# Input projection of a decoder layer: pairs of weight tiles, units of two row blocks, accumulators in three banks

## Chip, cores and metric

One NeuronCore of a Trainium2 chip runs the whole program. The metric is device microseconds of one execution. The time before is 1057.71 us, the median of three runs (1054.66 to 1057.97).

## The reference

One layer of a hybrid decoder, batch 1, 256 tokens, model width 2048, float32. A vector c gives six modulation vectors (shift, scale and gate for two sub-layers) through a matrix of 2048 x 12288. The normed and modulated input h goes through one input projection `w_in` of 2048 x 5144. Its columns feed four groups of eight heads of width 64: A (dilated windows), B (sliding window, two key heads, sinks), C (block sparse), D (compressed, selected and window attention with gates, two key heads). At 256 tokens these are causal attentions with different biases and masks. Each group's output is normed, the four are joined and go through the output projection `w_out` (2048 x 2048), gated into x. Then a router picks two of 16 experts (width 512) for each token, and a final norm follows.

```
mod = silu(c) @ ada_w + ada_b                  # sh1, sc1, g1, sh2, sc2, g2
h   = rmsnorm(x) * (1 + sc1) + sh1
q_a,k_a,v_a, q_b,k_b,v_b, q_c,k_c,v_c, q_d,k_dc,v_dc,k_ds,v_ds,k_dw,v_dw, g_d = split(h @ w_in)
x   = x + g1 * (concat(rmsnorm(o_a), rmsnorm(o_b), rmsnorm(o_c), rmsnorm(o_d)) @ w_out)
x   = x + g2 * moe(rmsnorm(x) * (1 + sc2) + sh2)
out = rmsnorm(x)
```

## The kernel before

All weights stream once from HBM as units of 512 KB (128 partitions x 1024 floats) through one list. `Stream` (L101) gives each unit the next free slot of a ring of 11 slots, to which two more are added when an attention group's bias tile is done (L990) and more when the attention's pool is closed (L1133). SyncE's queue issues all of these loads in the list's order; each waits until the former user of its slot is done.

**First stage.** Eight rounds (L606 to L634). Each round loads eight units of `ada_w` for sc1 and sh1 (256 columns, rows of 1 KB) and two early units of `w_in` (one row block of 128 rows by 1024 columns, rows of 4 KB, L253). It makes two row blocks of h as a high and a low half (`Hh`, `Hl`, L599), and multiplies the early units into four accumulators, D's first four tiles. A product in two halves is three matmuls (`three`, L534): low weight x high h, high x low, high x high. The weight's halves are made by `halves` (L555): a cast on ScalarE (L560) and a subtraction on VectorE (L562). Two more accumulators, "S" and "pv" (L565), take tile 4 (D's window keys) and three quarters of tile 6 (C's first keys); one unit of 4 row blocks x 256 columns of one of the two is loaded in each round but the first (L274 to L277).

**Second stage.** The input projection's other tiles, each of 256 columns as four units of 4 row blocks x 256 columns (rows of 1 KB, L205). The tiles' order is written out by hand (`wtiles`, L192): D's gates, then for C and for A the keys, values and queries of the first 256 columns and the same of the second, then B. One tile accumulates in one "mm" bank of PSUM, two in turn (L696). A unit is 24 matmuls of 256 columns: for keys and queries the weight is the stationary side (L537 to L539), for values h is (L541 to L543). After the last unit the tile is copied out by ScalarE (`evac`, L726). Between these units stand 96 units of `ada_w` of 4 KB rows that VectorE accumulates (`ada_acc_v`, L477, L484), spread over the list by L285 to L294.

The four attentions are generators. After each unit of the projection `step(PACE[m])` (L1087) adds a fraction to a credit; each whole point runs the front generator to its next yield (L1019). One full step of an attention (L978) computes scores of one item, transposes the probabilities of the item before and multiplies the values of the one before that. D's generator is queued at the first piece, the others behind the last unit of the first query tile of their group (L1088), and each waits where its second query tile is not yet there (L980).

**Output projection.** 32 units of `w_out` of 512 columns (L1212), three matmuls each for the halves, with the gate g1's 32 units of `ada_w` between them. Each unit lets `step(3)` run, so B's attention ends here. `WORDER` (L42) puts the twelve units of D, C and A for two column blocks ahead of B's first. At the fifth unit `attention_done` (L1124) closes the attention's buffers; loads into their memory wait for B's end. Then come the router, the gather (L1375) and eight pairs of experts.

The change touches `wtiles` and `win_units` (L192 to L208), the first stage (L274, L580 to L590, L626 to L637), `pieces`, `piece_mms` and `evac` (L652 to L762), the order of the first copies out and the queueing of the attentions (L1071, L1088) and `PACE` (L51).

## Time and profile before

| | us |
|---|---|
| median of three runs | 1057.71 |
| the profiled execution's own time | 1057.37 |
| its span, first to last instruction | 1055.6 |
| TensorE busy | 961.1 (91%) |
| VectorE busy | 499.2 (47%) |
| ScalarE busy | 350.0 (33%) |
| bytes moved | 371.18 MB, mean 352 GB/s |

How to read it: PE is TensorE's matmuls, PEld its weight loads, DVE is VectorE, ACT ScalarE, SP the queue of SyncE. A matmul's busy time contains its way through the pipeline, so matmuls overlap and their starts tell the pace. PEclk is the granted share of TensorE's clock. The DMA share is the mean busy share of 16 engines; it can read a little over 1. "idle before, releaser" is the time an instruction's engine stood idle ahead of it, and what ended it. A line such as L173 belongs to a helper that all matmul groups of a batch use, so groups are told apart by their tiles: `acc` is the input projection, `oacc` the output projection, `sp`, `PT` and `opv` are scores, transposes and values, `ada` modulation.

### The profile page before, as it was taken

How to read it: one execution, taken by the hardware profiler on the slowest of the kernel's cores; microseconds unless marked ns; L12 is line 12 of the kernel's file. 1: busy time of each engine (PE TensorE's matmuls, PEld its weight loads, DVE VectorE, ACT ScalarE, POOL GpSimd, SP SyncE). 2: the span in 40 equal slices, each digit the busy share in tenths (PEclk: the TensorE clock that was granted, in tenths of full speed). 3: DMA queues.
4: the chain of work that ended last, by engine and by line, in shares of the span. 5: the costliest groups of instructions: out<-in, count | busy, mean ns of one | idle time of the engine just before them, and what ended most of it. 6: DMA issues, size and time to landing. Idle time of an engine off the chain costs nothing.

```text
span 1055.6 us, 16579 instructions
## 1 busy us (share of the span) xinstructions
PE 961.1 (91%) x6433; PEld 581.7 (55%) x6433; DVE 499.2 (47%) x1008; ACT 350.0 (33%) x763; POOL 4.8 (0%) x14
## 2 busy tenths in 40 slices
PE   5899989999899998989998999999989897998884
PEld 1677778898788985646794435433343232432222
DVE  2444466996898998344444232414033130413115
ACT  3333345566776757534443101100020000200013
POOL 0000000000000000000000000000000000000000
PEclk9999999999999999989998999999999999999998
DMA  9999999996999999889743999999999999999994
GB/s 330 357 357 357 351 307 348 348 371 213 348 325 346 347 375 384 311 283 377 277 163 123 410 408 409 409 409 409 410 409 409 409 409 409 409 410 409 409 386 137
DMA packets 172031, 371.18 MB, mean 352 GB/s; under 512 B 13561, under 2 KB 92322, under 8 KB 171690
## 3 DMA queue, kind: packets, MB, share of 16 engines
q1 hardware_dynamic: 170944, 368.42, 95.0%
q10 hardware_dynamic: 938, 1.61, 0.4%
q8 instruction: 53, 0.87, 0.4%
q14 instruction: 32, 0.26, 0.1%
q0 software_dynamic: 64, 0.02, 0.0%
HBM read 367.91 MB, written 2.10 MB: 351 GB/s over the span
## 4 chain that ended last, share of the span: by engine, by line
PE 47%; DMA 37%; DVE 8%; ACT 4%; issue 3%; SPq 0%; ACTq 0%; DVEq 0%
DMA ugu<-in_exp_w_gate_dram 11%; DMA ugu<-in_exp_w_up_dram 10%; DMA udh<-in_exp_w_down_dram 6%; PE dn L170 6%; DMA uw<-in_w_in_dram 4%; PE acc L537 4%; PE acc L538 4%; PE acc L539 3%; PE ada L170 3%; DMA usc<-in_ada_w_dram 3%; PE oacc L541 3%; PE pg L1384 3%; PE oacc L543 3%; PE oacc L542 3%; PE gatep L170 2%
## 5 line engine op out<-in xcount | busy, mean ns | idle before, releaser
L537 PE MATMUL acc<-Hh,wlo 128*128 128x256 f32 x512 | 145.0, 293 | 7.3 <-DVE wlo L562 4.7
L538 PE MATMUL acc<-Hl,whi 128*128 128x256 f32 x512 | 145.2, 286 | 0.0
L539 PE MATMUL acc<-Hh,whi 128*128 128x256 f32 x512 | 144.4, 285 | 0.0
L173 PE MATMUL gatep<-ugu,xg 128*64 128x512 f32 x364 | 123.1, 600 | 0.0
L173 PE MATMUL upp<-ugu,xg 128*64 128x512 f32 x368 | 121.5, 596 | 0.0
L170 PE MATMUL dn<-udh,heT 128*64 128x512 f32 x242 | 112.1, 600 | 2.9 <-DVE heT L1454 2.6
L173 PE MATMUL dn<-udh,heT 128*64 128x512 f32 x234 | 108.3, 600 | 0.0
L537 PEld LDWEIGHTS acc<-Hh,wlo 128*128 128x128 f32 x512 | 95.6, 191 | 18.1 <-DVE wlo L562 7.7
L538 PEld LDWEIGHTS acc<-Hl,whi 128*128 128x128 f32 x512 | 97.8, 191 | 3.5 <-issue 3.0
L539 PEld LDWEIGHTS acc<-Hh,whi 128*128 128x128 f32 x512 | 97.7, 191 | 2.7 <-issue 2.3
L1437 DVE TENSOR_TENSOR he<-upp,sg 128x128 f32<-128x128 f32 x32 | 7.1, 284 | 171.0 <-PE upp L173 168.3
L562 DVE TENSOR_TENSOR wlo<-uw,whi 128x1024 fp32r<-128x1024 f32 x62 | 75.7, 1221 | 19.2 <-ACT whi L560 19.2
L170 PE MATMUL gatep<-ugu,xg 128*64 128x512 f32 x144 | 75.4, 612 | 7.8 <-DMA ugu<-in_exp_w_gate_dram 7.7
L170 PE MATMUL upp<-ugu,xg 128*64 128x512 f32 x144 | 73.9, 601 | 7.5 <-DMA ugu<-in_exp_w_up_dram 7.5
L560 ACT CAST whi<-uw 128x1024 fp32r<-128x1024 f32 x62 | 64.9, 1048 | 45.4 <-DMA uw<-in_w_in_dram 18.4
L1516 ACT CAST yhl<-yo 128x512 fp32r<-128x512 f32 x31 | 19.2, 618 | 159.5 <-DVE yo L1510 153.2
L1467 DVE TENSOR_TENSOR xt<-xt,sco 128x512 f32<-128x512 f32 (+1 forms) x70 | 42.3, 639 | 54.7 <-PE sco L1466 54.3
L170 PEld LDWEIGHTS dn<-udh,heT 128*64 128x64 f32 x242 | 30.0, 136 | 62.1 <-issue 48.8
L562 DVE TENSOR_TENSOR wlo<-uo,whi 128x1024 fp32r<-128x1024 f32 x31 | 37.8, 1223 | 51.0 <-ACT whi L560 51.0
L1433 ACT ACTIVATE sg<-gatep 128x512 f32<-128x512 f32 x8 | 4.8, 597 | 162.4 <-PE gatep L173 162.4
L541 PE MATMUL oacc<-wlo,Oh 128*128 128x512 f32 (+1 forms) x160 | 58.5, 367 | 0.1
L543 PE MATMUL oacc<-whi,Oh 128*128 128x512 f32 (+1 forms) x160 | 56.5, 353 | 0.0
(396 smaller groups left out, 1777.1 us busy)
## 6 DMA issues: line engine op xcount, KB each, us to landing
ugu<-in_exp_w_up_dram SPq DMA_DIRECT2D x128, 512.0 KB, 10.2
ugu<-in_exp_w_gate_dram SPq DMA_DIRECT2D x127, 512.0 KB, 10.2
udh<-in_exp_w_down_dram SPq DMA_DIRECT2D x119, 512.0 KB, 10.2
usc<-in_ada_w_dram SPq DMA_DIRECT2D x64, 512.0 KB, 8.6
ush<-in_ada_w_dram SPq DMA_DIRECT2D x62, 512.0 KB, 7.1
uw<-in_w_in_dram SPq DMA_DIRECT2D x62, 512.0 KB, 6.8
ug<-in_ada_w_dram SPq DMA_DIRECT2D x56, 512.0 KB, 7.0
uo<-in_w_out_dram SPq DMA_DIRECT2D x31, 512.0 KB, 9.1
```

Of the source, the lines that this page charges most:

```text
L170: ins = op(*args, **kw).ins
L173: ins = op(*args, **kw).ins
L537: ins = mm(o, wl, hh, start=first, stop=False)
L538: mm(o, wh, hl, start=False, stop=False)
L539: mm(o, wh, hh, start=False, stop=last)
L541: ins = mm(o, hh, wl, start=first, stop=False)
L542: mm(o, hl, wh, start=False, stop=False)
L543: mm(o, hh, wh, start=False, stop=last)
L560: A.copy(hi, w)
L562: V.tensor_tensor(lo, w, hi[:].bitcast(F32), OP.subtract)
L1384: mm(pg[:, i, :], x_[:, t, i, 128 * c:128 * c + 128], oh4[q][:, t].rearrange("p e s -> p (e s)"), start=n == 0, stop=n == 3)
L1467: V.tensor_tensor(y(t, cs), y(t, cs), o, OP.add)
```

## The change

The tiles of C, A and B's queries become pairs of 512 columns, loaded as eight units of 2 row blocks x 512 columns (rows of 2 KB). A pair has two accumulators, one for each 256 columns of keys or queries, or for each 128 tokens of values; a value unit is then 12 matmuls of 512 columns. Accumulators take the banks "ada", "mm", "mm" in turn. C's keys, one unit in each of the eight rounds, take the place of tiles 4 and 6 in the first stage; D's window keys (four units of rows of 1 KB, like B's keys) come behind the gates. A pair's first tile is copied out ahead of the second's matmuls of the last unit. An attention is queued behind the last unit of its query pair. The pace goes from 0.65 to 0.7 for C and from 0.5 to 0.45 for A.

```
-PACE = {"D": 0, "C": 0.65, "A": 0.5, "B": 0.8}
+PACE = {"D": 0, "C": 0.7, "A": 0.45, "B": 0.8}
...
-              ("D", "kw", 0, 4864), ("D", "g", 0, 5120)]
-    for m, q0 in (("C", 2304), ("A", 0)):
-        for j in range(2):
-            wtiles += [(m, kind, j, q0 + off + 256 * j) for kind, off in (("k", 512), ("v", 1024), ("q", 0))]
-    wtiles += [("B", "kb", 0, 2048), ("B", "q", 0, 1536), ("B", "q", 1, 1792)]
+              ("C", "k", None, 2816), ("D", "g", 0, 5120), ("D", "kw", 0, 4864),
+              ("C", "v", None, 3328), ("C", "q", None, 2304),
+              ("A", "k", None, 512), ("A", "v", None, 1024), ("A", "q", None, 0),
+              ("B", "kb", 0, 2048), ("B", "q", None, 1536)]
+
+    def wparts(i):
+        return 1 if wtiles[i][1] == "g" else 8 if wtiles[i][2] is None else 4
...
+        n = wparts(i)
+        kn, w = 16 // n, 64 * n
         def mk(u):
             return lambda t: nc.sync.dma_start(
-                t.rearrange("p (k n) -> p k n", k=4), winT[:, 4 * u:4 * u + 4, col:col + 256])
-        return [((("w", i), u), mk(u)) for u in range(4)]
+                t.rearrange("p (k n) -> p k n", k=kn), winT[:, kn * u:kn * u + kn, col:col + w])
+        return [((("w", i), u), mk(u)) for u in range(n)]
...
-        if j % 2:
-            units.append(win_units(4)[j // 2])
-        elif j:
-            units.append(win_units(SIXTH)[j // 2 - 1])
+        units.append(win_units(NEARLY - 1)[j])
...
+    def early_mms2(u):
+        hi, lo = [a.rearrange("p (k n) -> p k n", k=2) for a in esp.pop(("pair", u))]
+        for i in range(2):
+            for cc in range(2):
+                c0 = 256 * i + 128 * cc
+                for kk in range(2):
+                    k = 2 * u + kk
+                    three(early[4 + i][:, cc, :], hi[:, kk, c0:c0 + 128], lo[:, kk, c0:c0 + 128],
+                          Hh[:, k, :], Hl[:, k, :], False, k == KC - 1 and cc == 1, True)
...
         if j:
             early_mms(2 * j - 1)
-        if j and j % 2 == 0:
-            early_mms5(4, j // 2 - 1)
+            early_mms2(j - 1)
         early_split(2 * j + 1)
...
+        early_split2(j)
     for k in (14, 15):
         early_mms(k)
-    early_mms5(4, 3)
+    early_mms2(7)
...
         if u == 0:
-            acc_banks[i] = ps("mm", [128, 2, 256], name="acc")
...
+            acc_banks[i] = []
+            for _ in range(tiles):
+                acc_banks[i].append(ps(("ada", "mm", "mm")[len(turn) % 3], [128, 2, 256], name="acc"))
+                turn.append(1)
+        for tj in range(tiles):
+            bank_ = acc_banks[i][tj]
+            if kind == "v":
+                ts = slice(128 * tj, 128 * tj + 128)
+                for kk in range(kn):
+                    k = kn * u + kk
+                    three(bank_[:].rearrange("p c n -> p (c n)"), hv[:, kk, :], lv[:, kk, :], Hh[:, k, ts], Hl[:, k, ts],
+                          k == 0, k == KC - 1, False)
+            else:
...
+                        ins = three(bank_[:, cc, :], hv[:, kk, c0:c0 + 128], lv[:, kk, c0:c0 + 128], Hh[:, k, :], Hl[:, k, :],
+                                    first, k == KC - 1 and cc == 1, True)
...
+            if u == nu - 1:
+                evac(i, tj)
...
-    for i in (2, 0, 1, 3, 4):
-        evac(i)
+    for i, tj in ((2, 0), (4, 1), (0, 0), (1, 0), (3, 0), (4, 0)):
+        evac(i, tj)
...
-            if u == 3 and wtiles[i][1:3] == ("q", 0) or pn == 1:
+            if u == 7 and wtiles[i][1] == "q" or pn == 1:
                 side.append(attention(m))
```

## Rows read from the trace of the kernel before

**Rows 1.** Windows by stage: us, busy by engine (instructions), PEclk, DMA share, GB/s
```profile
0.00:150.00 150.00, 127.25 (x1451) 90.27 (x1451) 64.08 (x161) 53.62 (x107) 2.05 (x9) 0.99 1.04 341
160.00:400.00 240.00, 231.19 (x1968) 204.72 (x1968) 208.58 (x380) 153.94 (x367) 1.05 (x2) 1.00 0.97 336
400.00:550.00 150.00, 140.63 (x813) 98.76 (x811) 73.85 (x141) 71.77 (x150) 1.70 (x3) 0.97 0.84 298
...
580.00:1030.00 450.00, 414.51 (x1886) 157.48 (x1884) 114.01 (x228) 42.93 (x72) 0.00 (x0) 0.99 1.03 407
```

**Rows 2.** Narrower windows, the same columns
```profile
50.00:100.00 50.00, 47.39 (x562) 35.58 (x561) 22.97 (x52) 17.48 (x34) 0.00 (x0) 1.00 1.08 356
...
400.00:430.00 30.00, 26.11 (x146) 16.46 (x144) 19.80 (x51) 19.36 (x54) 0.00 (x0) 0.94 1.04 382
...
470.00:480.00 10.00, 10.00 (x41) 4.02 (x34) 1.79 (x2) 2.10 (x4) 0.00 (x0) 0.74 1.03 388
...
560.00:570.00 10.00, 10.00 (x44) 4.58 (x45) 4.32 (x11) 2.77 (x5) 0.00 (x0) 0.81 0.01 2
```

**Rows 3.** Timeline of TensorE in the input projection: start us, us, instruction
```profile
257.81 0.28 PE L537 MATMUL acc<-Hh,wlo 128*128 128x256 f32 x1
257.93 0.28 PE L538 MATMUL acc<-Hl,whi 128*128 128x256 f32 x1
```

**Rows 4.** Waits of TensorE, 160 to 400 us, three largest: total us, times, longest
```profile
PE acc L537 <- DVE wlo L562: 4.7, 5, 1.7
PE PT L173 <- ACT prob L932: 1.0, 1, 1.0
PE acc L541 <- DVE wlo L562: 1.0, 1, 1.0
```

**Rows 5.** Groups by line and form, 160 to 460 us: busy, mean ns, idle before, releasers
```profile
L562 DVE TENSOR_TENSOR wlo<-uw,whi 128x1024 fp32r<-128x1024 f32 x54 | 65.9, 1221 | 17.9 <-ACT whi L560 17.9
...
L560 ACT CAST whi<-uw 128x1024 fp32r<-128x1024 f32 x54 | 56.5, 1047 | 43.3 <-DMA uw<-in_w_in_dram 18.4 <-PE acc L539 11.4 <-issue 3.7
```

**Rows 6.** Timeline of TensorE in the output projection
```profile
437.89 0.40 PE L541 MATMUL oacc<-wlo,Oh 128*128 128x512 f32 x1
438.12 0.39 PE L542 MATMUL oacc<-whi,Ol 128*128 128x512 f32 x1
```

**Rows 7.** Timeline of TensorE around one attention step
```profile
406.70 0.33 PE L170 MATMUL PT<-ident,prob 128*128 128x128 f32 x1
406.87 0.71 PE L173 MATMUL PT<-ident,prob 128*128 128x128 f32 x5
407.50 0.93 PE L173 MATMUL sp<-qkB 64*128 64x128 f32 x8
408.36 0.62 PE L170 MATMUL ada<-ug,cB 128*32 128x512 f32 x1
...
409.36 0.43 PE L170 MATMUL opv<-probT,vB 128*64 128x256 f32 x1
...
410.16 0.50 PE L541 MATMUL oacc<-wlo,Oh 128*128 128x512 f32 x1
```

**Rows 8.** Timelines of TensorE, then VectorE: B's attention, the projection's end
```profile
389.69 0.37 PE L170 MATMUL sp<-qkB 64*128 64x128 f32 x1
...
400.38 0.28 PE L539 MATMUL acc<-Hh,whi 128*128 128x256 f32 x1
...
425.69 0.93 PE L173 MATMUL sp<-qkB 64*128 64x128 f32 x8
...
433.54 0.93 PE L173 MATMUL sp<-qkB 64*128 64x128 f32 x8
...
462.60 1.43 DVE L1103 TENSOR_TENSOR Ol<-oT,Oh 128x256 fp32r<-128x256 f32 x4
```

**Rows 9.** Timeline of TensorE behind the twelfth output unit
```profile
465.99 0.37 PE L1147 MATMUL bb<-wbs,ones 128*128 128x16 f32 x2 [1.84 <-DVE wbs L1145]
469.75 1.06 PE L170 MATMUL ada<-ug,cB 128*32 128x512 f32 x1 [3.39 <-DMA ug<-in_ada_w_dram]
```

More of the change, by code (lines that the diff above doesn't have):

```diff
@@ L36 @@
 NEARLY = 5
-SIXTH = 6
 ATAG = "ada"
@@ L655, in hybrid_trunk_kernel @@
             continue
-        if kind == "g":
-            pieces.append((i, 0))
-        else:
-            pieces += [(i, u) for u in range(3 * (i == SIXTH), 4)]
+        pieces += [(i, u) for u in range(wparts(i))]
     split_out = {}
@@ L666, in split @@
             stream.done(key)
-    acc_banks = {SIXTH: early[5]}
+    acc_banks, turn = {}, []
     evacuated = set()
```

76 lines of the change are left out of this document (28 added, 48 removed).

## The prediction

> **What bounds the kernel now.** I read the stages first [rows 1]. The reader is to see four regimes. From 0 to 150 us the DMA share is 1.04 while TensorE has gaps: the first stage is bound by loads. From 160 to 400 us, the input projection with the attention woven in, TensorE is busy 231.19 of 240 us, the DMA engines 0.97 and VectorE 208.58: three resources are nearly full, TensorE most. From 400 to 550 us the output projection leaves the DMA at 0.84. From 580 us on the experts run at a DMA share of 1.03 and 407 GB/s. Between 560 and 570 us the DMA stands still (share 0.01) because every slot is full [rows 2]; so expert loads wait for the router, whatever the loads before them did. A change ahead of the router shows at the end of the kernel only as far as it brings the TensorE chain up to 550 us forward; 550 us to the end is a constant here.
>
> Busy time of a pipelined TensorE can hide small gaps, so I checked the spacing of the starts. The projection's matmuls of 256 columns start every 0.12 us [rows 3], 24 in a unit, 2.88 us a unit. What TensorE waits for in 160 to 400 us is short: 4.7 + 1.0 us for the low half of a weight, at most 1.0 us for any result of the attention, nothing for an accumulator being copied out [rows 4]. So this stage runs at the speed of TensorE, with at most 240 - 231.19 = 8.8 us of waiting to win. The low half waits for the high half, 17.9 us in all, and the high half's idle time of 43.3 us was ended by a weight load for 18.4 us of it [rows 5]: loads are late, but far more of their lateness is swallowed in the queues than reaches TensorE.
>
> **The change, part by part.** The sum is made against the profiled execution's own time, 1057.4 us (span 1055.6); the median shown, 1057.7, is 0.3 us above it.
>
> Values as matmuls of 512 columns. The value tiles of C and A are 16 units. Before, a unit is 24 matmuls at 0.12 = 2.88 us. After, it is 12 of 128x512; the output projection has that form, with starts 0.23 us apart [rows 6], so 2.76 us. That is 0.12 x 16 = **1.9 us** off TensorE's path.
>
> One unit more in the first stage (8 of C's keys for 4 + 3 before), one fewer after it. TensorE's work of 2.88 us leaves the stage that it bounds: **-2.9 us**. In the first stage its 24 matmuls and the two splits lie under the loads. What counts there is load time. In 50 to 100 us the core reads 356 GB/s [rows 2]; each of the eight rounds there has 8 modulation units and one input unit with rows of 1 KB and two early units with rows of 4 KB. A unit of 0.524 MB takes 0.524/0.407 = 1.29 us at the experts' rate (4 KB rows) [rows 1]; eleven at 356 GB/s take 16.2 us, so nine with 1 KB rows take 13.6, or 1.51 us each. A row of 512 columns is 2 KB; the stretch where only such rows move, 400 to 430 us, shows 382 GB/s [rows 2], 1.37 us a unit. So 8 x 1.37 - 7 x 1.51 = **+0.4 us**. If that cover went, the unit would cost its 2.9 us of matmuls there; bounds 0 to +2.9.
>
> Rows of 2 KB in 48 of the 56 units left after the first stage (D's window keys and B's keys keep rows of 1 KB): 0.14 us each, 6.7 us less load time. It counts only where a load ends last. Bounds: 0 (TensorE sets the pace anyway) to 8.8 us (all of its idle time). Of the 5.7 us that TensorE waits for a low half [rows 4], the load stands behind about half (18.4 of 43.3 [rows 5]). I take **-3.0 us**, near the waits that the trace names.
> The 356 GB/s of the 1 KB stretch is at once what a rule would call the end. The Trainium skill (DMA: Bandwidth & Descriptors, Where 436 GB/s comes from) says that loads from HBM are bound by the HBM side at about 358 GB/s a core; by it longer rows win nothing. The 382 and 407 GB/s of this trace speak against that, so the sum goes by the rows.
>
> Three accumulator banks in turn. No row shows TensorE waiting for a copy out of an accumulator between tiles [rows 4], so I cost it at nothing. The cover: the pair's first tile opens a bank that was emptied at least a tile ago, and its 12 matmuls (1.4 us) stand ahead of the second's. If ScalarE is late, each of seven tile changes could cost about one cast of 1.05 us [rows 5]; bounds 0 to +7.
>
> Order of the tiles and the pace. D's window keys come after the gates, and attention steps are paid at 0.7, 0.45 and 0.8 a unit. Counting the generator's steps through both orders, 35 are taken before the last unit now and 31 after the change; comparing the points reached, B's first three steps move from the last four units to behind the last unit, since B's generator is only appended there. A full step is 1.66 us of TensorE for six transposes and eight score matmuls (406.70 to 408.36) and 0.80 us for eight value matmuls (409.36 to 410.16) [rows 7], 2.5 us. For TensorE this is a move of 7.4 us from one full stage to the next and sums to nothing; VectorE and ScalarE get room in the stage where they are full and lose it where they have plenty.
>
> But B's chain gets late relative to the output projection. Now its first scores start at 389.69, 10.9 us ahead of the end of the input projection at 400.6, and its last result is written at 464.03 [rows 8]: 63.4 us after that end. Twelve output units need D, C and A alone; then B's are needed, and TensorE already waits there: 1.84 us for VectorE and 3.39 us for a load at 469.75 [rows 9], because SyncE's queue stands behind buffers that B's attention frees. After the change the first scores come no sooner than the last tile's copies, about 1.5 us behind the end. Upper bound: the chain keeps its 74.3 us, and ends 76 us after it, **12.4 us** later than now. Lower bound: four score steps follow each other at the shortest distance seen, 433.54 - 425.69 = 7.9 us, then the 30.5 us from the last scores to the result: 55.7 us, less than the 63.4 now, so 0. The long distances, 18 us, are those that lay in the end of the input projection, where VectorE was full; that speaks for the low end. I take **+2.0 us**.
>
> SyncE issues one descriptor set per unit as before, 64 input units in all; copies out of the accumulators are the same or fewer. Both zero, hidden under the units' 2.9 us.
>
> Sum: -1.9 - 2.9 + 0.4 - 3.0 + 2.0 = -5.4, so 1057.4 - 5.4 = **1052.0 us**. About 0.3% (3.2 us) is what a measurement of this kernel can tell from no change.
>
> **The rivals.** (1) B's attention is late: the place is the output projection behind its twelfth unit, the price the upper bound, 10.4 us more than I took, and it decides as soon as B's last result comes over 63.4 us after the input projection's end. The clock adds to it: behind the gap that ends at 469.75 the granted clock is 0.74 over 470 to 480 us [rows 2], ten us in part at the lower of its two levels, and a second gap like it would cost up to 0.26 x 10 = 2.6 us. Time 1052.0 + 10.4 + 2.6 = 1065.0, slower. For it: TensorE waits at this very place now. Against: VectorE and ScalarE are half idle there [rows 1].
> The Trainium skill (TensorE: Matmul & The Clock Gate, HAM oscillation — how this bites in real kernels) says likewise that a wait for a load between bursts lets the next burst run at the lower clock.
> (2) Rows of 2 KB move no faster here than the 356 GB/s of the 1 KB stretch, or no load was ever last: the 3.0 us go, and the unit more in the first stage costs 0.524/0.356 = 1.5 us for 0.4. Time 1052.0 + 3.0 + 1.1 = 1056.1: no change. For it: TensorE is already full, and the stage's mean, 336 GB/s, lies under 356 [rows 1].
> This is the case that the bound of 358 GB/s in the Trainium skill (DMA: Bandwidth & Descriptors, Where 436 GB/s comes from) would give.
> (3) The full gain: all 8.8 us of idle time go and B costs nothing: 1052.0 - 5.8 - 2.0 = 1044.2. For it: the largest sum of waits of TensorE there is for weights [rows 4]; against: no more than half of them leads back to a load [rows 5].
> (4) The third bank does not take waits away but adds them (the pair's second bank is copied out too late): up to +7 us, 1059.0; no wait of this kind is in the trace.
>
> **How the numbers follow.** The forecast's case has 0.45, the full gain 0.17, the unchanged cases (2) and (4) 0.20, B's late chain 0.18. Faster: 0.45 + 0.17 = 0.62; same 0.20; slower 0.18. The range runs from a microsecond under the full gain, 1043, to 1062, which holds three quarters of the 13 us of rival 1.
>
> **What would show it.** Right: projection units of the value tiles with 12 matmuls at 0.23 us; the weight loads of 2 KB at over 356 GB/s in 160 to 390 us; the last projection matmul some 12 to 15 us sooner than 400.6 (2.9 + 1.9 + 3.0 from the edits, and most or all of the 7.4 us of moved steps, less 0.4), and the router and the experts about 5 us sooner. Wrong: TensorE's idle time of 160 to 400 us unchanged; or a gap of over 5 us behind the twelfth output unit, with the first scores of B to its last result still 74 us long. If the input projection ends that much sooner and the router no sooner, rival 1 has it.

## The result, and the profile after

The changed kernel is slower: 1065.9 us (median of 6 runs, 1063.24 to 1070.06) against 1056.0 us before on the same chip (6 runs, 1053.07 to 1057.97). The ratio is 1.0089, with a 95% interval of 1.0073 to 1.0105. The profiled execution took 1064.03 us, with a span of 1062.2 us; the span of before is 1055.6. The prediction had 1052.0, faster, and its range ended at 1062.

The stages by windows, with the columns of [rows 1]:

```profile
0.00:150.00 150.00, 131.05 (x1481) 95.06 (x1482) 67.68 (x164) 55.18 (x108) 2.05 (x9) 1.00 1.04 347
...
160.00:400.00 240.00, 224.72 (x1713) 190.07 (x1713) 209.93 (x359) 148.07 (x337) 1.06 (x2) 0.96 0.95 340
400.00:550.00 150.00, 139.50 (x813) 96.33 (x812) 70.53 (x153) 80.70 (x180) 1.68 (x3) 0.98 0.79 277
580.00:1030.00 450.00, 414.48 (x1884) 159.06 (x1882) 111.89 (x225) 42.29 (x71) 0.00 (x0) 0.98 1.02 406
```

Against [rows 1] the expert stage is the same (406 GB/s for 407). The loss lies ahead of 550 us. From 160 to 400 us TensorE is busy 224.72 us for 231.19: it idles 15.3 us instead of 8.8, and its granted clock is 0.96 instead of 1.00. VectorE is busy 209.93 us there, as before (208.58), though steps of the attention have moved out.

The ends of the stages, as the timeline of TensorE has them (here the last matmul of the projection, then the last of the output projection):

```profile
404.21 0.28 PE L541 MATMUL acc<-Hh,whi 128*128 128x256 f32 x1
...
555.61 0.28 PE L545 MATMUL oacc<-whi,Oh 128*128 128x256 f32 x1
```

and the last of the output projection in the kernel before (that of its projection is in [rows 8]):

```profile
548.52 0.28 PE L543 MATMUL oacc<-whi,Oh 128*128 128x256 f32 x1
```

The projection's last matmul ends at 404.49, where the prediction wanted some 12 to 15 us sooner than 400.6. The output projection's ends at 555.89; before it was 548.8. So 3.8 us are lost by the end of the projection, and 3.3 more behind it; from there the offset stays (the span is 6.6 us longer).

What TensorE waited for from 160 to 400 us, in the form of [rows 4]:

```profile
PE ada_c L500 <- DVE ada_v L486: 6.1, 3, 2.9
PE rr L1010 <- DVE dg L1009: 3.1, 1, 3.1
...
PE acc L539 <- DVE wlo L564: 0.9, 3, 0.5
PE acc L543 <- DVE wlo L564: 0.8, 2, 0.4
```

The waits for a weight's low half fell from 5.7 us to 1.7. New waits for VectorE took their place, at two kinds of small matmuls: the columns of a finished modulation sum (`ada_c`) and the last step of an attention (`rr`). The worst place, on TensorE:

```profile
357.55 0.50 PE L1002 MATMUL ssqp<-ones,ssum 128*128 128x1 f32 x4
361.11 1.20 PE L1010 MATMUL rr<-dg,ones 128*128 128x128 f32 x4 [3.06 <-DVE dg L1009]
365.25 1.08 PE L500 MATMUL ada_c<-ada_v,ones 128*32 128x256 f32 x8 [2.94 <-DVE ada_v L486]
366.38 0.58 PE L539 MATMUL acc<-Hh,wlo 128*128 128x256 f32 x1
366.76 0.41 PE L540 MATMUL acc<-Hl,whi 128*128 128x256 f32 x1
366.98 0.41 PE L541 MATMUL acc<-Hh,whi 128*128 128x256 f32 x1
...
371.03 0.28 PE L539 MATMUL acc<-Hh,wlo 128*128 128x256 f32 x1
```

and on VectorE at the same time:

```profile
358.16 1.28 DVE L486 SCALAR_TENSOR_TENSOR ada_v<-ug,cT,ada_v 128x1024 f32<-128x1024 f32 x1
359.37 0.16 DVE L377 RECIPROCAL rb<-rs_s 128x2 f32<-128x2 f32 x1
359.48 1.28 DVE L486 SCALAR_TENSOR_TENSOR ada_v<-ug,cT,ada_v 128x1024 f32<-128x1024 f32 x1
360.69 0.48 DVE L1009 TENSOR_SCALAR dg<-ident,rb 128x128 f32<-128x128 f32 x2
361.08 1.28 DVE L486 SCALAR_TENSOR_TENSOR ada_v<-ug,cT,ada_v 128x1024 f32<-128x1024 f32 x1
362.34 1.65 DVE L1013 SCALAR_TENSOR_TENSOR oT<-oT,gT,rr 128x256 f32<-128x256 f32 x4
363.92 1.28 DVE L486 SCALAR_TENSOR_TENSOR ada_v<-ug,cT,ada_v 128x1024 f32<-128x1024 f32 x1
365.11 2.35 DVE L564 TENSOR_TENSOR wlo<-uw,whi 128x1024 fp32r<-128x1024 f32 x2
```

VectorE has no gap here. The short `dg` that TensorE needs for `rr` stands behind two modulation sums of 1.28 us each; the columns `ada_c` need a sum that itself stands behind `oT`. On TensorE the projection's matmuls stand behind these small ones in the order of its instructions, and start after them. The next rows show what that leaves behind (windows, the same columns):

```profile
290.00:300.00 10.00, 9.66 (x61) 7.31 (x62) 9.77 (x19) 6.98 (x19) 0.00 (x0) 1.00 1.03 404
...
360.00:370.00 10.00, 5.89 (x29) 4.75 (x30) 9.89 (x15) 0.76 (x1) 0.00 (x0) 0.54 0.93 343
...
470.00:480.00 10.00, 3.95 (x24) 1.20 (x26) 5.25 (x12) 1.99 (x2) 1.68 (x3) 0.67 0.74 242
```

From 360 to 370 us the granted clock is 0.54 and ScalarE does almost nothing (0.76 us). Behind the stall the projection's matmuls start 0.22 us apart (366.76, 366.98) where they started 0.12 us apart before it: near the lower of the two levels, 1.2 for 2.4 GHz. A stall is paid twice, as idle time and as slow matmuls: from 366.38 to 371.03, 21 projection matmuls take 4.65 us where 0.12 each would make 2.5, some 2.1 us on top of the 6.0 us of the two waits. The Trainium skill (TensorE: Matmul & The Clock Gate, HAM oscillation — how this bites in real kernels) says that a wait between bursts lets the next burst run slower; these rows agree in kind.

In the output projection the places of [rows 9] come 6.7 us later, with one wait more (timeline of TensorE):

```profile
469.39 0.67 PE L413 MATMUL perm<-pkc,ident 128*64 128x128 f32 x8 [1.84 <-DVE oT L1013]
472.67 0.36 PE L1152 MATMUL bb<-wbs,ones 128*128 128x16 f32 x2 [2.61 <-DVE wbs L1150]
476.48 1.06 PE L169 MATMUL ada<-ug,cB 128*32 128x512 f32 x1 [3.44 <-DMA ug<-in_ada_w_dram]
```

B's attention, the prediction's term of +2.0, can be read off directly. Its first scores (TensorE) and its last result (VectorE):

```profile
404.42 0.37 PE L169 MATMUL sp<-qkB 64*128 64x128 f32 x1
...
469.36 1.42 DVE L1108 TENSOR_TENSOR Ol<-oT,Oh 128x256 fp32r<-128x256 f32 x4
```

The chain is 66.4 us long (74.3 before) and ends 66.3 us behind the projection's last matmul (63.4 before [rows 8]): 2.9 us later than it was.

Two parts of the change did what was forecast. A value unit's matmuls of 512 columns start 0.23 us apart (median 0.231 over the projection, 0.120 for 256 columns):

```profile
180.82 0.40 PE L543 MATMUL acc<-wlo,Hh 128*128 128x512 f32 x1
181.06 0.40 PE L544 MATMUL acc<-whi,Hl 128*128 128x512 f32 x1
181.29 0.39 PE L545 MATMUL acc<-whi,Hh 128*128 128x512 f32 x1
```

And C's keys end with the first stage (copies by ScalarE, each released by TensorE's last product of the tile):

```profile
156.99 0.37 ACT L750 COPY qkC<-acc 128x256 f32<-128x256 f32 x1 [1.76 <-PE acc L541]
157.26 0.38 ACT L751 COPY qkC<-acc 128x256 f32<-128x256 f32 x1
158.41 0.37 ACT L750 COPY qkC<-acc 128x256 f32<-128x256 f32 x1 [0.77 <-PE acc L541]
```

Loads reach 404 GB/s from 290 to 300 us, in the window above; in the kernel before, the fastest such 10 us between 160 and 400 us had 386. But that window mixes rows of 2 KB with modulation units of 4 KB rows, and over the whole stage the rate went from 336 to 340 GB/s only.

The last product of the first stage is done by 158.41; before, it was 158.0. The projection's matmuls run on without a gap to 161.25, ahead of D's gates; these 24 are the first unit of D's window keys, which are counted in the second stage.

### The profile page after: what moved, and what is told of

It reads as the page before. It is cut to its first block, busy times and chain, and to the rows that moved or that the text cites. A ratio compares the mean times of both kernels' runs of the same rounds, so it can differ in the third digit from the quotient of the medians.

```text
span 1062.2 us, 16220 instructions
## 1 busy us (share of the span) xinstructions
PE 964.6 (91%) x6241; PEld 578.7 (54%) x6241; DVE 502.8 (47%) x1008; ACT 352.6 (33%) x761; POOL 4.8 (0%) x14
## 4 chain that ended last, share of the span: by engine, by line
PE 60%; DMA 25%; DVE 7%; ACT 4%; issue 2%; SPq 1%; DVEq 0%; ACTq 0%
DMA ugu<-in_exp_w_up_dram 15%; PE dn L169 8%; PE acc L539 6%; PE acc L540 5%; PE acc L541 5%; PE ada L169 4%; DMA ugu<-in_exp_w_gate_dram 4%; DMA udh<-in_exp_w_down_dram 3%; PE oacc L543 3%; PE upp L169 3%; PE oacc L544 3%; PE pg L1389 3%; PE oacc L545 3%; PE gatep L169 3%; DVE wlo L564 2%
## 5 line engine op out<-in xcount | busy, mean ns | idle before, releaser
L539 PE MATMUL acc<-Hh,wlo 128*128 128x256 f32 x512 | 148.3, 299 | 2.5 <-ACT Hh L608 1.5
L540 PE MATMUL acc<-Hl,whi 128*128 128x256 f32 x512 | 148.3, 292 | 0.6 <-DVE Hl L609 0.6
L541 PE MATMUL acc<-Hh,whi 128*128 128x256 f32 x512 | 148.1, 291 | 0.0
L539 PEld LDWEIGHTS acc<-Hh,wlo 128*128 128x128 f32 x512 | 99.4, 198 | 15.1 <-issue 6.3
L540 PEld LDWEIGHTS acc<-Hl,whi 128*128 128x128 f32 x512 | 101.2, 198 | 3.4 <-issue 1.3
L541 PEld LDWEIGHTS acc<-Hh,whi 128*128 128x128 f32 x512 | 101.0, 197 | 3.2 <-issue 3.1
L169 PE MATMUL gatep<-ugu,xg 128*64 128x512 f32 x144 | 75.2, 611 | 10.7 <-DMA ugu<-in_exp_w_gate_dram 10.5
```

Source lines behind the costliest of these rows:

```text
L169: ins = op(*args, **kw).ins
L539: ins = mm(o, wl, hh, start=first, stop=False)
L540: mm(o, wh, hl, start=False, stop=False)
L541: mm(o, wh, hh, start=False, stop=last)
```

## The experiments

All runs in one table. The ratio is to the kernel before, run beside it on the same chip; differences in us below are differences of ratios times 1057 us. "Steps left" are the attention steps that remain for the output stage behind the last projection unit, counted by taking the generators through the list of units by hand. These are places in the program's list; where the instructions stand on TensorE can differ, as the fifth round shows. (The counts of steps in the projection, in the expectations, contain one to three pieces of D's compression that the units otherwise take by themselves.) "Projection" is the end of its last matmul, "output stage" the time from there to the output projection's last matmul, both in the profiled execution alone, which lies up to 5 us off its kernel's median. Busy and clock are TensorE's from 150 to 550 us.

| kernel | us | ratio, 95% interval | steps left | projection | output stage | busy of 400 | clock |
|---|---|---|---|---|---|---|---|
| before | 1056.0 | 1 | 4 | 400.7 | 148.2 | 381.8 | 0.99 |
| after | 1065.9 | 1.0089 (1.0073 to 1.0105) | 7 | 404.5 | 151.4 | 374.2 | 0.97 |
| a_pace_back | 1079.5 | 1.0214 (1.0198 to 1.0229) | 7 | 401.9 | 169.4 | 366.2 | 0.95 |
| b_pace_new | 1063.3 | 1.0055 (1.0041 to 1.0069) | 4 | 418.6 | 140.3 | 380.4 | 0.96 |
| first_old | 1071.7 | 1.0139 (1.0120 to 1.0158) | 7 | 415.4 | 150.6 | 370.3 | 0.96 |
| second_old | 1053.8 | 0.9970 (0.9957 to 0.9983) | 4 | 407.7 | 137.0 | 380.1 | 0.98 |
| single_late | 1070.6 | 1.0137 (1.0106 to 1.0169) | 7 | 412.5 | 148.9 | 370.9 | 0.96 |
| two_banks | 1066.7 | 1.0090 (1.0059 to 1.0121) | 7 | 415.0 | 149.1 | 371.3 | 0.95 |
| q_single | 1068.3 | 1.0108 (1.0084 to 1.0132) | 6 | 407.1 | 156.4 | 370.7 | 0.95 |
| delay3 | 1080.0 | 1.0218 (1.0192 to 1.0244) | 7 | 413.2 | 160.7 | 365.7 | 0.95 |
| light_before | 1048.1 | 0.9917 (0.9899 to 0.9934) | 4 | 399.4 | 138.8 | 386.0 | 0.99 |
| light_after | 1051.4 | 0.9944 (0.9927 to 0.9962) | 7 | 392.7 | 152.2 | 379.6 | 0.98 |
| second_pace | 1061.3 | 1.0029 (1.0012 to 1.0046) | 5 | 418.5 | 138.0 | 376.8 | 0.97 |
| best_v | 1050.3 | 0.9937 (0.9920 to 0.9954) | 4 | 400.8 | 140.5 | 377.7 | 0.99 |
| pairs_ahead | 1059.7 | 1.0016 (0.9994 to 1.0037) | 4 | 410.5 | 140.3 | 377.6 | 0.98 |
| pairs_dpace | 1063.2 | 1.0061 (1.0037 to 1.0085) | 7 | 408.2 | 147.3 | 374.4 | 0.97 |
| bq_single | 1066.7 | 1.0090 (1.0066 to 1.0113) | 6 | 402.9 | 153.5 | 372.9 | 0.97 |
| best_v_late | 1067.0 | 1.0102 (1.0070 to 1.0135) | 6 | 406.6 | 151.9 | 370.6 | 0.97 |
| cq_pair | 1052.0 | 0.9951 (0.9937 to 0.9965) | 4 | 407.0 | 137.8 | 379.7 | 0.98 |
| akq_pair | 1056.7 | 0.9985 (0.9973 to 0.9998) | 4 | 410.8 | 140.7 | 378.1 | 0.98 |

**First round: stage against stage, and the pace.** The first reading of the two traces was theory 1: the 24 matmuls up to 161.25 were taken for the first stage's, and VectorE for the limit of the projection.

a_pace_back, the kernel after with the old pace:
```
-PACE = {"D": 0, "C": 0.7, "A": 0.45, "B": 0.8}
+PACE = {"D": 0, "C": 0.65, "A": 0.5, "B": 0.8}
```


> The kernel after, with the pace of the attention steps put back to 0.65 for C and 0.5 for A (0.7 and 0.45 after). Theory 1 (one unit more in the first stage lies bare there, 3.2 us; the input projection gains nothing because VectorE, not TensorE, is full in it; the attention comes out later, 2.8 us, through the order of the tiles): the two paces nearly cancel (8 and 12 units at +0.05 each way), so the time stays within 2 us of the after's 1065.9, and the last input-projection matmul stays at 404 to 405 us. Rival P (the new pace alone pushes attention steps to the wrong place): at least half of the 9.9 us between the two kernels comes back, 1056 to 1061.

Measured 1.0214: slower still, by 13 us. Neither had it. The pace works through the places that it gives the steps, and with A at 0.5 the queue of steps runs empty twice ahead of B's, so nothing is gained for the output stage (169.4 us).

b_pace_new, the kernel before with the new pace (the same line, turned round):

> The kernel before, with the new pace (0.7 for C, 0.45 for A). Theory 1: within 2 us of the before's 1056.0. Rival P: 1061 to 1066.

Measured 1.0055, 5.8 us: rival P, here. The pace alone costs the old tiles more than half of what the whole change costs, and the projection's end slips from 400.7 to 418.6. It gives the pairs back 13 us. So a pace belongs to an order of tiles.

first_old, the kernel after with the first stage of before:
```
-              ("C", "k", None, 2816), ("D", "g", 0, 5120), ("D", "kw", 0, 4864),
-              ("C", "v", None, 3328), ("C", "q", None, 2304),
+              ("D", "kw", 0, 4864), ("D", "g", 0, 5120), ("C", "k", 0, 2816),
+              ("C", "v", None, 3328), ("C", "k", 1, 3072), ("C", "q", None, 2304),
...
-        units.append(win_units(NEARLY - 1)[j])
+        if j % 2:
+            units.append(win_units(4)[j // 2])
+        elif j:
+            units.append(win_units(SIXTH)[j // 2 - 1])
```


> The kernel after with the first stage of before: D's window keys and three quarters of C's first key tile are loaded and multiplied there, C's second key tile goes back to the input projection, the rest stays by pairs with three banks and the new pace. Theory 1: the last matmul of the first stage comes back from 161.2 to about 158 us, 3.2 us; of the input projection one unit more of 2.9 us of TensorE is not the bound, so the time is 1065.9 - 3 = 1063 (1061 to 1064), still slower than before by 5 to 8 us. Rival S (the pairs, the banks and the order of the second stage cost nothing; the first stage has it all): 1056 to 1058. Rival Q (the first stage's extra unit is paid back in the second stage, as the sum of the prediction has it): no change or slower, 1066 to 1069.

Measured 1.0139: 5.3 us slower than the kernel after, where theory 1 wanted 3 us faster. It is rival Q's direction, the prediction's own sum (the unit more in the first stage is won back), though 1071.7 lies above its range; the attention steps also stand up to three units elsewhere in this list. The copies of C's keys (above) bear the direction out: the first stage is 0.4 us longer, not 3.

second_old, the new first stage with the old second stage:
```
-              ("C", "v", None, 3328), ("C", "q", None, 2304),
-              ("A", "k", None, 512), ("A", "v", None, 1024), ("A", "q", None, 0),
-              ("B", "kb", 0, 2048), ("B", "q", None, 1536)]
+              ("C", "v", 0, 3328), ("C", "q", 0, 2304), ("C", "v", 1, 3584), ("C", "q", 1, 2560)]
+    for j in range(2):
+        wtiles += [("A", kind, j, off + 256 * j) for kind, off in (("k", 512), ("v", 1024), ("q", 0))]
+    wtiles += [("B", "kb", 0, 2048), ("B", "q", 0, 1536), ("B", "q", 1, 1792)]
...
-                acc_banks[i].append(ps(("ada", "mm", "mm")[len(turn) % 3], [128, 2, 256], name="acc"))
+                acc_banks[i].append(ps("mm", [128, 2, 256], name="acc"))
...
-PACE = {"D": 0, "C": 0.7, "A": 0.45, "B": 0.8}
+PACE = {"D": 0.65, "C": 0.65, "A": 0.5, "B": 0.8}
...
-            if u == 7 and wtiles[i][1] == "q" or pn == 1:
+            if u == 3 and wtiles[i][1:3] == ("q", 0) or pn == 1:
```
(and the code for single value tiles, as before.)

> The kernel after with its new first stage (all eight units of C's keys there) but the input projection in single tiles of 256 columns, two accumulator banks, the old pace, and the attention queued behind the first query tile. Theory 1: the first stage ends at 161 us as after, the single tiles cost no time against the pairs, the output stage is as before: 1056.0 + 3.2 = 1059 (1057 to 1061). Rival S (all of it is the first stage): 1064 to 1067. Rival Q (the extra unit is paid back in the second stage): 1055 to 1057.

Measured 0.9970: 3.2 us faster than before, below even rival Q's range. Theory 1 falls for the first stage, and rival S too. By these two runs the new first stage is worth 3 to 5 us (the 3 is the cleaner figure: counted from the list's end, the steps of second_old stand where they stood before), and the second stage as changed (tiles, order, pace) costs 12.6 us.

**Second round: order or form.**

single_late, that second stage with its single tiles put into the pairs' order, attention queued behind the second query tile, new pace:
```
-              ("C", "v", 0, 3328), ("C", "q", 0, 2304), ("C", "v", 1, 3584), ("C", "q", 1, 2560)]
-    for j in range(2):
-        wtiles += [("A", kind, j, off + 256 * j) for kind, off in (("k", 512), ("v", 1024), ("q", 0))]
+              ("C", "v", 0, 3328), ("C", "v", 1, 3584), ("C", "q", 0, 2304), ("C", "q", 1, 2560)]
+    for kind, off in (("k", 512), ("v", 1024), ("q", 0)):
+        wtiles += [("A", kind, j, off + 256 * j) for j in range(2)]
...
-            if u == 3 and wtiles[i][1:3] == ("q", 0) or pn == 1:
+            if u == 3 and wtiles[i][1:3] == ("q", 1) or pn == 1:
```


> The new first stage, new pace and all positions of the attention steps as in the kernel after (values ahead of both query tiles, attention queued behind the second query tile), but each tile single: units of 4 row blocks of 256 columns, values as matmuls of 256 columns, two accumulator banks. Against the kernel with single tiles in the old order (1053.8) this moves only the order and the pace; against the kernel after (1065.9) it changes only the tiles' form. Theory 2 (the pairs cost because a pair's queries are finished only with both tiles, so the attention starts later, bunches, and TensorE meets VectorE's and ScalarE's backlog in order): 1063 to 1071. Rival F (the form of the pairs itself, their bursts, their banks, the 512-column values): 1053 to 1058.

Measured 1.0137, theory 2. No pair is left in its second stage, and it loses 17.7 us against second_old. Order, queueing and pace have the loss; against it the kernel after, with its pairs, is 5 us faster, with an uncertainty of some 4.

two_banks, the kernel after without the third bank:
```
-                acc_banks[i].append(ps(("ada", "mm", "mm")[len(turn) % 3], [128, 2, 256], name="acc"))
+                acc_banks[i].append(ps("mm", [128, 2, 256], name="acc"))
```


> The kernel after with two accumulator banks in turn for the pairs, without the third. Theory 2 and the prediction's term of zero: a pair's first bank was emptied 1.4 us of matmuls before, six pair changes by at most one copy of about 1 us each: 1066 to 1072. Rival K (the third bank, taken from the modulation's accumulators, is what makes the modulation late, with the three waits at its columns of 6.1 us): faster, 1055 to 1061.

Measured 1.0090, the ratio of the kernel after. The third bank makes no difference that this run can tell (its interval is 3.3 us either way); rival K is out.

q_single, the kernel after with single query tiles and the attention behind the first:
```
-              ("C", "v", None, 3328), ("C", "q", None, 2304),
+              ("C", "v", None, 3328), ("C", "q", 0, 2304), ("C", "q", 1, 2560),
...
-            if u == 7 and wtiles[i][1] == "q" or pn == 1:
+            if u == 3 and wtiles[i][1:3] == ("q", 0) or pn == 1:
```
(A's and B's queries likewise.)

> The kernel after with the query tiles of C, A and B loaded and multiplied one by one, the attention queued behind the first of them as before; keys and values stay by pairs. The attention of C and A starts four units earlier than in the kernel after (it is still later than before, where the second key and value tiles came behind the first queries), B's starts ahead of the last tile. Theory 2: half or more of the loss comes back, 1055 to 1061. Rival F: 1064 to 1068, since the keys and values keep their form.

Measured 1.0108: no gain, a miss for theory 2 as I had put it. The count says why: with the new pace, D's steps still stand ahead of C's in the queue, so C's first step stays at unit 34 and A's at 48. Queueing sooner moves nothing in the list while the queue is full, but for one step of B; only the pace does.

delay3, the modulation's column step three units later:
```
-DELAY = 1
+DELAY = 3
```


> The kernel after with the modulation's column step (the transposition of VectorE's sums by TensorE) put three units behind the sum instead of one. Theory W (what TensorE loses is above all the in-order wait at these columns, 2.9 + 1.8 + 1.4 us, and the lower clock behind each): 1056 to 1061, with no wait of over 0.5 us at the columns and the granted clock of 360 to 370 us near 1. Theory 2: these waits are one face of VectorE's backlog and another wait takes their place: 1063 to 1068.

Measured 1.0218, with a_pace_back the slowest of all, and above both expectations. The waits at the columns shrink from 6.1 to 1.8 us, and TensorE waits for low halves instead (its largest waits, 160 to 420 us):

```profile
PE acc L539 <- DVE wlo L564: 11.4, 6, 5.8
PE ada_c L500 <- DVE ada_v L486: 1.8, 1, 1.8
```

Theory W falls. The wait named in the profile is only where VectorE's backlog met TensorE; taken away there, it comes back larger at another operand from VectorE (11.4 us at L539, 0.9 in the kernel after).

**Third round: relieve VectorE, part the pace from the order, and a faster kernel.**

light_before and light_after, half of each modulation sum left out on VectorE, in both kernels:
```
-            V.scalar_tensor_tensor(acc, w, cT[:, u:u + 1], acc[:], OP.mult, OP.add)
+            V.scalar_tensor_tensor(acc[:, 0:512], w[:, 0:512], cT[:, u:u + 1], acc[:, 0:512], OP.mult, OP.add)
```


> The kernel before with VectorE's modulation sums on half of the columns (the other half of these sums is left out; all loads stay), some 50 us of VectorE's work less between 160 and 410 us. If VectorE is what TensorE stumbles over there, TensorE's gaps of 160 to 400 us (8.8 us) mostly go: 1046 to 1053. If VectorE never counts: 1055 to 1058.

> The kernel after with the same half of VectorE's modulation sums left out. Theory V (the changed order and pace cost time because they bunch VectorE's work, and TensorE waits in order behind it; with VectorE relieved the change's own gain of some 5 to 7 us of TensorE work stands alone): not slower than the kernel before with the same part left out, 1042 to 1050, with TensorE's gaps of 160 to 400 us under 8 us. Rival C (the loss lies in the attention's own chain, TensorE to VectorE to ScalarE and back, or in loads): still 6 us or more slower than the kernel before with the same part left out.

Measured 0.9917 and 0.9944: light_before came as expected, light_after 1.4 us above its range, between theory V and rival C; its gaps of 160 to 400 us are 8.6 us, where theory V wanted under 8. The distance between the two shrinks from 0.89% to 0.27%, so about two thirds of the loss went with VectorE's work; by the runs' intervals it could be half or nearly all. Where it goes is plain in the stages. Windows of 160 to 400 and 400 to 550 us, of the kernel before so relieved:

```profile
160.00:400.00 240.00, 234.47 (x2000) 206.65 (x1994) 176.63 (x403) 160.45 (x386) 1.06 (x2) 1.00 1.00 355
400.00:550.00 150.00, 141.47 (x800) 100.70 (x801) 73.06 (x156) 74.11 (x152) 1.89 (x3) 0.96 0.78 277
```

and of the kernel after:

```profile
160.00:400.00 240.00, 231.44 (x1792) 194.01 (x1791) 176.01 (x391) 159.64 (x376) 1.06 (x2) 0.99 0.97 359
400.00:550.00 150.00, 138.13 (x807) 97.92 (x806) 67.39 (x142) 73.15 (x151) 1.68 (x3) 0.97 0.75 263
```

With VectorE at 176 us instead of 209 (33 us less, not the 50 expected), the changed projection ends at 392.7, 11.8 us sooner than with its full load, the old one only 1.3 us sooner. Now, and only now, the change has its gain in the projection: 6.7 us (392.7 against 399.4). The output stage takes it back: 152.2 us against 138.8. The pair is not quite clean: with less work on VectorE the attention also stands elsewhere on TensorE (in light_before B's first scores start at 378.13, in before at 389.69 [rows 8]).

second_pace, second_old with 0.7 and 0.45:

> The kernel with the new first stage and single tiles in the old order (1053.8), with the new pace 0.7 and 0.45 for C and A. It tells the order from the pace: single tiles in the pairs' order with the new pace took 1070.6. Theory 2 (the order costs, the pace little): 1053 to 1060. Rival P (the pace has most of it): 1063 to 1071.

Measured 1.0029: 6 us of the 17.7 between second_old and single_late are the pace of C and A. The rest is the order together with the later queueing and D's pace of 0, which single_late has and this run has not. It lies between the two expectations, as both have a part.

best_v, second_old with only the values as pairs:
```
-              ("C", "v", 0, 3328), ("C", "q", 0, 2304), ("C", "v", 1, 3584), ("C", "q", 1, 2560)]
-    for j in range(2):
-        wtiles += [("A", kind, j, off + 256 * j) for kind, off in (("k", 512), ("v", 1024), ("q", 0))]
+              ("C", "v", None, 3328), ("C", "q", 0, 2304), ("C", "q", 1, 2560),
+              ("A", "k", 0, 512), ("A", "v", None, 1024), ("A", "q", 0, 0), ("A", "k", 1, 768), ("A", "q", 1, 256)]
```


> The kernel with the new first stage and single tiles in the old order and pace (1053.8), with only the values of C and A as pairs of tiles (2 row blocks of 512 columns, matmuls of 512 columns), C's and A's values ahead of the first queries; keys and queries single. Sum: 16 units with 0.12 us less, 1.9 us; C's and A's attention start four units later each. Theory 2: the gain is about given back, 1052 to 1060. If the pairs' form has its full worth (4.7 us between the single tiles and the pairs in the pairs' order): 1048 to 1051.

Measured 0.9937, where the pairs' form has its full worth: 6.7 us faster than before, 3.5 us faster than second_old. This is the fastest kernel that computes the whole result. Its attention did not start later: C's and A's first steps stay at units 32 and 46 of the list, since the queue ahead of them decides.

**Fourth round: the same tiles, other places for the steps.**

pairs_ahead, all tiles of C and A in pairs with three banks as in the kernel after, the steps at the units of best_v by the list:
```
-PACE = {"D": 0, "C": 0.7, "A": 0.45, "B": 0.8}
+PACE = {"D": 0.65, "C": 0.65, "A": 0.5, "B": 0.8}
...
-              ("B", "kb", 0, 2048), ("B", "q", None, 1536)]
+              ("B", "kb", 0, 2048), ("B", "q", 0, 1536), ("B", "q", 1, 1792)]
...
-            if u == 7 and wtiles[i][1] == "q" or pn == 1:
+            if u == 7 and wtiles[i][1] == "q" or u == 3 and wtiles[i][:3] == ("B", "q", 0) or pn == 1:
```
pairs_dpace is its first edit alone, bq_single its second and third alone.

> The kernel after, pairs and all three banks, but with attention steps also on the units of D's window keys (0.65) and with 0.65 and 0.5 for C and A, and B's queries as two single tiles with its attention queued behind the first. Counted through the generators, every attention step then lies at the same unit as in the fast kernel with only the values as pairs (35 steps in the projection, 4 left; 30 and 7 in the kernel after). Theory L (the loss is the lateness of the attention steps against the units, whatever the tiles' form): 1046 to 1053. Rival F2 (keys and queries in pairs, or the third bank, cost by themselves): 1058 or more.

> The same with B's queries left as a pair, so that B's attention still comes behind the last unit: D's, C's and A's steps lie two to three units earlier than in the kernel after, B's where they are there (7 left). If B's late chain is the loss (rival 1 of the prediction): 1060 to 1066. If the loss is D's, C's and A's steps: 1048 to 1056.

> The kernel after with only B's queries as two single tiles and B's attention queued behind the first of them: the other half of the same table. D's, C's and A's steps stay late, one B step comes ahead of the projection's end. Rival 1: 1054 to 1061. Theory L with D, C and A late: 1063 to 1069.

Measured 1.0016, 1.0061 and 1.0090, beside 1.0089 with neither edit. B sooner alone wins nothing; D, C and A sooner wins 3 us, hardly clear of the noise; both win 7.7 us. So neither half is the loss by itself: pairs_dpace has the time that rival 1 gave it, bq_single the one that theory L gave it. pairs_ahead brings back half of the way to best_v and lies in the range of rival F2; its 12 runs go from 1053.4 to 1063.0. The output stage answers as theory L has it (140.3 us with 4 steps left, 147.3 with 7); the projection does not (410.5, against 400.8 in best_v).

best_v_late, best_v with the pace of the kernel after:
```
-PACE = {"D": 0.65, "C": 0.65, "A": 0.5, "B": 0.8}
+PACE = {"D": 0, "C": 0.7, "A": 0.45, "B": 0.8}
```


> The fastest kernel so far (values in pairs, keys and queries single, 1050.3) with the pace of the kernel after: 0 on D's window keys, 0.7 and 0.45. Nothing but the place of the steps changes: 31 in the projection and 6 left instead of 35 and 4. Theory L: 1062 to 1070. Rival F2 (the form of the tiles decides): 1050 to 1055.

Measured 1.0102, theory L: 17.4 us lost with not one tile, load or matmul changed. Windows of best_v, then of best_v_late:

```profile
160.00:400.00 240.00, 227.36 (x1765) 190.75 (x1758) 210.79 (x379) 156.08 (x366) 1.06 (x2) 0.99 0.96 340
400.00:550.00 150.00, 141.05 (x828) 100.86 (x827) 76.77 (x168) 77.60 (x166) 1.68 (x3) 0.98 0.83 299
```

```profile
160.00:400.00 240.00, 222.52 (x1687) 186.90 (x1679) 204.59 (x352) 144.43 (x333) 1.05 (x2) 0.98 0.94 327
400.00:550.00 150.00, 138.80 (x801) 95.86 (x801) 74.03 (x158) 80.29 (x177) 1.68 (x3) 0.95 0.85 296
```

Two steps fewer stand in the projection by the list, and the others come later: on TensorE A's four scores start at 349 to 400 us, in best_v at 326 to 373. TensorE is busy 4.8 us less up to 400 us, yet the projection ends 5.8 us later (406.6), not sooner. Then the output stage is 11.4 us longer, with TensorE's waits in it up from 4.9 to 11.2 us.

**Fifth round: keys and queries in pairs, with the steps at the same units of the list.** cq_pair is best_v with C's queries as a pair, akq_pair best_v with A's keys and queries as pairs, for instance:
```
-              ("C", "v", None, 3328), ("C", "q", 0, 2304), ("C", "q", 1, 2560),
+              ("C", "v", None, 3328), ("C", "q", None, 2304),
```


> The fastest kernel so far (values of C and A in pairs, 1050.3, ratio 0.9937) with C's queries as a pair too; every attention step stays at its unit. All pairs with the steps at the same units, and a third bank, took 1059.7 (ratio 1.0016). Theory E (keys and queries in pairs cost by their own form, since both tiles' banks are copied out in one go and the unit's matmuls come in another order): a share by the number of tiles, one of four, ratio 0.995 to 0.997. Rival K (it is one coincidence, at A's tiles or at the third bank): ratio 0.992 to 0.995.

> The fastest kernel so far with A's keys and queries as pairs and C's queries single; every attention step stays at its unit. Theory E: two of four pairs, ratio 0.997 to 0.999. Rival K with A's tiles as its place: ratio 0.999 to 1.003. If both runs stay at 0.992 to 0.995, the cost lies in the third bank or in B's place.

Measured 0.9951 and 0.9985, both within theory E, the first on its edge with rival K: 1.5 and 5 us. The first lies within the interval of best_v, the second does not; the two losses add up to 6.6 us, and pairs_ahead, which has both and the third bank besides, is 8.4 us behind best_v.

But the steps are at the same units in the list only. The first scores of A on TensorE, in best_v, then in akq_pair:

```profile
325.64 0.37 PE L169 MATMUL sp<-qkA 64*128 64x128 f32 x1
```

```profile
360.43 0.37 PE L169 MATMUL sp<-qkA 64*128 64x128 f32 x1
```

In akq_pair they stand behind the last unit of A's queries, as the pair's tiles are finished only there. So A's attention starts 35 us later (in pairs_ahead 24 us, in best_v_late 24 us), while in cq_pair, which costs little or nothing, it starts 5.5 us later. So these runs do not part theory E from lateness, theory L. Whether the pairs' own form costs anything besides (the copies of both banks in one go, the order of the products) was not tried apart and stays open.

## Why the prediction was wrong, step by step

**The step that failed** is "Order of the tiles and the pace", with the premise that it rests on, "this stage runs at the speed of TensorE". It moved three attention steps of 7.4 us of TensorE out of the projection and called that "a move of 7.4 us from one full stage to the next" that "sums to nothing", since VectorE and ScalarE would get room in the stage where they are full. The number of steps moved was right (7 left for 4; by the list 30 and not 31 stand ahead of the end). The price was not. In the forecast's own terms the projection was to end 12 to 15 us sooner and the output stage to take 9.4 us longer (7.4 moved, 2.0 for B). The projection ended 3.8 us later and the output stage took 3.3 us longer, so the miss of 16 to 19 us lies in the projection. best_v_late leaves two steps more behind the projection in just that way, puts the others one to four units of the list later, keeps everything else, and costs 17.4 us; single_late, which changes the order too, 17.7.

Two things were missing in it. First, the projection does not get shorter when TensorE has less to do there. The premise "this stage runs at the speed of TensorE", with "at most 8.8 us of waiting to win", was read off one schedule in which TensorE's and VectorE's queues happened to fit. VectorE had 208.58 of 240 us to do [rows 1], and it has 204 to 211 us in both kernels and in best_v and best_v_late. TensorE's waits for VectorE, from 160 us to the projection's end, sum to 11.3 us in the kernel after for 6.1 before, and to 9.7 in best_v_late for 6.5 in best_v, with the clock falling behind the worst of them. That fewer attention matmuls between the units bring TensorE to VectorE's results too soon is how I read this. light_after supports it: relieve VectorE, and the gain of the projection that I had forecast appears, 6.7 us beside light_before; it is smaller than the 12 to 15 us of the forecast. Second, against any kernel but the one before, what is moved out is paid in full in the output stage, and more: with 4 or 5 steps left that stage took 137 to 141 us in all but the kernel before (148.2, with the stalls of 3.5 us at 420.6 and 3.4 at 469.8); with 6 or 7 left, 147 to 169. Two more steps are 5 us of TensorE by the prediction's own 2.5 us, but best_v_late's output stage grew by 11.4. The runs do not add up part by part: first stage (-3.2), values (-3.5) and lateness (+17.4) make +10.7 for a measured +9.4, and a further 6.6 us for keys and queries in pairs would not fit; if that cost is lateness too, it is in the 17.4 already.

**Values, -1.9.** Right: the starts are 0.231 us apart, so a unit takes 12 x 0.231 instead of 24 x 0.120 us, and 16 units save 1.7; second_old to best_v gained 3.5 us, with an uncertainty that takes this in.

**First stage, -2.9 and +0.4.** Right, as far as the runs tell. The stage's last product came 0.4 us later, and the unit saved behind it is worth 3 to 5 us by two pairs of runs. The trace alone misled me here until first_old spoke against it.

**Rows of 2 KB, -3.0.** Wrong in effect. The loads did get somewhat faster: in the trace a packet of 2 KB occupies its DMA engine for 91 ns on average (160 to 400 us, after), two of 1 KB for 101 ns (before). And the waits for low halves fell by 4.0 us. The Trainium skill (DMA: Bandwidth & Descriptors, Where 436 GB/s comes from) has about 358 GB/s as what binds loads from HBM; another of its pages (HBM Reference, Specifications (TRN2)) keeps that for two cores streaming at once and gives about 425 for a core alone. The 404 of this trace, from 290 to 300 us on one core with rows of 2 and 4 KB, agree with the second. But TensorE's waits moved to other results that VectorE owed, and their sum rose. Keys and queries in pairs were to gain nothing else, and in the fifth round they cost 1.5 and 5 us.

**Three banks, 0.** Right within 3.3 us (two_banks). Rival 4 has no part that these runs can tell.

**B's late chain, +2.0.** About right by its own measure: the last result of B comes 2.9 us later against the projection's end than before. The 12.4 us of the upper bound, with which rival 1 reckons, did not come: the chain got shorter, 66.4 us for 74.3. bq_single gained nothing. Only with D's, C's and A's steps put sooner is B's place worth more, 1.0061 less 1.0016, 4.8 us, with 2 us and more of uncertainty on each. That rival 1 named the time best (1065.0) is luck: its place, behind the twelfth output unit, does show waits of 1.84, 2.61 and 3.44 us and a clock of 0.67, but two of the three were there before, 1.84 and 3.39 us [rows 9], and over half of the loss was made ahead of it. One reading behind the +2.0 was wrong, too: of B's two long distances of 18 us, the second, 407.50 to 425.69 [rows 7, rows 8], lies behind the projection's end and not in it.

**Rivals 2 and 3**, 1056.1 and 1044.2, fell with the premise: the idle time of TensorE grew (15.3 us for 8.8) instead of staying or going.

What is not settled: why the kernel after reacts to 0.05 of pace by 13 us in the other direction than the single tiles do. The table says that its projection ends sooner (401.9) and its output stage takes 169.4 us; which of the waits there comes first was not tried.

## What to carry to other kernels

Where two engines are near full in one stage, the idle time of the fuller one is no measure of what can be won: halve the work of the other in an experiment, and see whether a saving appears at the stage's end. When an edit changes the order or the number of work units, side work that is paced by units moves with it; compare both kernels with the side work at the same places before judging the edit, and read these places from the trace: here a list that put them at the same units was not what ran on TensorE. An edit of several parts should be run in its parts: here two of them (values in pairs, C's keys in the first stage) make 1050.3 us, 0.6% faster than before, and the rest turned that into 0.9% slower.

## What the runs showed of the hardware that was not expected

Two waits of 3.06 and 2.94 us in the middle of dense matmuls cost about a third as much again behind them: 21 projection matmuls 0.22 us apart instead of 0.12, some 2.1 us, with a granted clock of 0.54 over 360 to 370 us. Over 150 to 550 us the mean clock was 0.99 in before and best_v, 0.97 in the kernel after, and 0.95 in a_pace_back and delay3, the slowest (and in two_banks and q_single).

The time is sensitive to the places of small work: 0.05 of pace, some attention matmuls a few units sooner or later, moved it by 6 to 13 us, more than any single saving of the change; and pairs_ahead and single_late spread over 9.6 and 9.2 us between their own runs, where the runs of before beside the others spread over 4 to 8.
